# Stick-breaking attention values: one 512-column matmul per key block in place of two of 256

## The chip, the cores and the metric

The kernel runs on one core of a Trainium2 chip. The metric is the device time of one execution in microseconds (us); the time before is the median of three runs. A core has five engines that work beside each other: PE (TensorE) multiplies matrices, DVE (VectorE) and ACT (ScalarE) do elementwise work, POOL (GpSimd) does elementwise work that need not read PSUM, and SP issues transfers. PEld is the loading of the stationary operand into PE, which the profile keeps apart from the matmuls (PE). PSUM is the memory that PE writes its sums to; SBUF is the working memory that all engines read.

## What is computed

One layer of a decoder: a feed-forward half step, a mixing step of two groups of heads side by side (HGRN2, a gated recurrence, and stick-breaking attention), an output projection, and a second feed-forward half step. The sequence is 1024 tokens behind 16 meta tokens, the width is 1024. The change is in the stick-breaking attention (8 heads of 64), which is strictly causal:

```python
z = einsum('bhqd,bhkd->bhqk', qblk, k) * scale
log_beta = where(allowed, log_sigmoid(z), -inf)
log_keep = where(allowed, log_sigmoid(-z), 0.0)
suffix = cumsum(log_keep, axis=3, reverse=True) - log_keep
w = exp(log_beta + suffix)
out = einsum('bhqk,bhkd->bhqd', w, v)
```

The last line is the part that changes: the weights `w` times the values `v`.

## The kernel before

Products that need more precision than one pass gives are made from two parts of each operand, a high part (a cast to the type float32r) and a low part (what the cast left over): high times high, high times low and low times high are summed, low times low is left out where it can be.

**The jobs.** The attention is cut into 32 jobs: 8 heads, and in each head four jobs of two query blocks of 128 (`b0` = 0, 6, 2, 4 is a job's first query block). A job has three lists of steps, each with a number that stands for its length on PE:

- `score`: the scores of a query block against its keys (tile `z`, lines 1205 to 1208), sigmoids on ACT (`keep`, `sig`), the suffix products by a scan on DVE (`keep`, line 1215), the weights by a multiplication on POOL (`sig`, line 1220);
- `turn`: PE transposes of the weights, one group of up to four key blocks at a time, into PSUM (tile `flip`, lines 1069 and 1118, two buffers). ACT casts each group to its high part and DVE subtracts for the low part (`sb_parts`, lines 1183 and 1184), into `wu` (groups of real keys) or `wm` (the 16 meta keys). A transpose into a buffer of `flip` waits until DVE has read that buffer;
- `value`: one step for each of the job's `b0` + 3 key blocks. The loaded operand `v` has 128 columns, 64 with the high part of the head's values and 64 with the low part. The high weights, 256 columns wide, move past all 128 columns (line 1139); the low weights move past the 64 high columns alone (line 1141). The sum `oacc` lies in PSUM, 256 columns wide; its partitions 0 to 63 have high times high and low times high, 64 to 127 have high weights times low values.

At a job's last key block `sb_out` takes the sum out: ACT copies partitions 64 to 127 (`olow`, line 1176), and one DVE addition of 64 x 256 (`ot`, line 1177) adds them to partitions 0 to 63. In each second head `put_split` then cuts the result into its parts (`ohi` on ACT, `olo` on POOL) and stores it.

**The order.** PE's order is as the program writes it. `braid` writes it in rounds: each round takes up a new job; a job's `turn` steps come two rounds and its `value` steps three rounds later. For each round the lengths of all its steps are summed, and blocks of other PE work (`fill`) are set between them until they come to 1.22 times that sum. The fill is 64 blocks of 12 matmuls each of the HGRN2 projections (tile `proj`, lines 160 to 162, 272, 384 or 512 columns wide). What is left of it runs after the last job. On DVE, ACT, POOL and SP the scheduler of the framework sets the order. Below, a block means one of these.

Of the kernel before, what the change touches and what calls it, by code (L numbers as in the profile page):

```python
# [11 lines left out]
F32 = mybir.dt.float32  # L12
F32R = mybir.dt.float32r
# [7 lines left out]
P = 128  # L21
# [3 lines left out]
META = 16  # L25
# [14 lines left out]
class Block:  # L40
# [1031 lines left out]
    def sb_jobs(self, keys, fetch, pool):  # L1072


        nc = self.nc
        qD, kD, vD, oD = keys
        pools = pool
        heads = [(p, hh) for p in range(4) for hh in range(2)]
        kept = {}

        def load(p, hh):
            rows = slice(64 * hh, 64 * hh + 64)
            qs = fetch.tile([P, SEQ], F32R, tag="qs", name="qs", bufs=2)
            ks = [fetch.tile([P, T], F32R, tag=f"ks{i}", name="ks", bufs=2) for i in range(2)]
            for i in range(2):
                part = slice(64 * i, 64 * i + 64)
                nc.sync.dma_start(qs.bitcast(F32)[part], qD[p, rows, i])
                for j in range(2):
                    nc.sync.dma_start(ks[j].bitcast(F32)[part], kD[p, rows, j])
            return qs, ks  # L1090

        def load_v(p, hh):
            v = fetch.tile([P, 9, P], F32R, tag="v", name="v", bufs=2)
            nc.sync.dma_start(v.bitcast(F32), vD[p, :, :, hh * P : (hh + 1) * P])
            return v

        def job(p, hh, qs, ks, v, b0):
            sigs, acc, wm, wu = [], [], [], []
            score, turn, value = [], [], []
            for bi in range(2):  # L1100
                score += self.sb_scores(pool, qs, ks, b0 + bi, sigs)

            def unit(u, bi):
                if bi == 0 or b0 == 4 * u - 1:
                    wu.append([
                        pool.tile([P, 4, 256], F32R, tag=f"wu{i}", name="wu", bufs=3)
                        for i in range(2)
                    ])
                spans = [(META + P * j, P) for j in range(4 * u, min(4 * u + 4, b0 + bi + 1))]
                ps = self.flip(sigs[bi], spans)  # L1110
                self.sb_parts([t[:, : len(spans), bi * P : (bi + 1) * P] for t in wu[u]], ps)

            def meta():
                wm.extend(kept["wm"][0])
                kept["wm"].reverse()
                ps = self.ptr.tile([META, 2, P], F32, tag="tr", name="flip")
                for bi in range(2):
                    nc.tensor.transpose(ps[:, bi, :], sigs[bi][:, :META], self.ident)
                self.sb_parts([t[:META] for t in wm], ps)

            for bi in range(2):
                for u in range(-(-(b0 + bi + 1) // 4)):
                    n = min(4, b0 + bi + 1 - 4 * u)
                    turn.append((107 * n, lambda u=u, bi=bi: unit(u, bi)))
            turn.append((214, meta))

            def values(j):
                if j == 0:
                    acc.append(self.po.tile([P, 256], F32, tag="o", name="oacc"))
                o = acc[0]  # L1130
                if j == b0 + 2:
                    w = [t.rearrange("p b t -> p (b t)") for t in wm]
                    vj, c = v[:, 0], slice(0, 256)
                else:
                    c = slice(128, 256) if j == b0 + 1 else slice(0, 256)
                    w = [t[:, j % 4, c] for t in wu[j // 4]]
                    vj = v[:, 1 + j]
                end = j == b0 + 2
                nc.tensor.matmul(o[:, c], vj, w[0], start=j == 0, stop=False,  # L1139
                                 skip_group_check=True)  # L1140
                nc.tensor.matmul(o[:64, c], vj[:, :64], w[1], start=False, stop=end,  # L1141
                                 skip_group_check=True)
                if end:
                    self.sb_out(p, hh, b0, o, kept, pool, oD)

            for j in range(b0 + 3):
                value.append((240, lambda j=j: values(j)))
            return score, turn, value

        kept["wm"] = [[fetch.tile([P, 2, P], F32R, name=f"wm{j}{i}") for i in range(2)]  # L1150
                      for j in range(2)]
        for t in chain(*kept["wm"]):
            nc.vector.memset(t.bitcast(F32), 0.0)
        none = kept["wm"][1][1].rearrange("p b t -> p (b t)").bitcast(F32)[META:]
        for p in range(4):
            nc.sync.dma_start(vD[p, META:, 0], none)
        ahead, v = load(*heads[0]), load_v(0, 0)
        yield None
        pool = pools[0]
        for i, (p, hh) in enumerate(heads):  # L1160
            qs, ks = ahead
            if i:
                v = load_v(p, hh)
            for b0 in (0, 6, 2, 4):
                if b0 == 2 and i + 1 < len(heads):
                    ahead = load(*heads[i + 1])
                yield job(p, hh, qs, ks, v, b0)

    def sb_out(self, p, hh, b0, o, kept, pool, oD):

        nc = self.nc
        if hh == 0 and b0 == 0:
            kept["o"] = pool.tile([P, SEQ], F32, tag="ot", name="ot")
        s = slice(b0 * P, b0 * P + 256)
        t = pool.tile([P, 256], F32, tag="olow", name="olow", bufs=2)
        nc.scalar.copy(t[64:], o[64:])
        nc.vector.tensor_add(kept["o"][64 * hh : 64 * hh + 64, s], o[:64], t[64:])
        if hh == 1:
            self.put_split(oD, p, s, kept["o"][:, s], pool)

# [643 lines left out]
```

## Time and profile before

| | before |
|---|---|
| three runs | 2082.09, 2081.91, 2078.43 us; median 2081.91 |
| the profiled execution's own time | 2077.59 us |
| its span | 2075.9 us |
| granted clock of PE, mean | 0.998 |
| the jobs lie at | about 914 to 1203 us of the span |
| high-weight matmuls into `oacc` | 160 from `wu` (32 of them 128 columns wide), 32 from `wm` |
| low-weight matmuls into `oacc` | as many |

The sum on the page counts every instruction's busy time, and matmuls overlap each other: a matmul of 256 columns is shown with 0.28 us, but the next can start about 0.11 us later. What a matmul costs in a row of others is therefore read from the distance between starts, not from its duration. "Idle" in brackets behind an instruction is the time that its engine stood still before it by the profile, with the work that ended it.

### The profile page before, as it was taken

To read this page: it belongs to the slowest core of one execution; us is meant where nothing else is said; L and a number is where in the kernel's file an instruction comes from. 1 tells how busy PE (TensorE), PEld (TensorE's weight loads), DVE (VectorE), ACT (ScalarE), POOL (GpSimd) and SP (SyncE) were. 2 spreads that over 40 slices of the span, in tenths; PEclk is the share of its full clock that TensorE was granted. 3 is DMA by queue.
4 is the path that set the end of the run, shared out by engine and by line. 5 is a ranking of instruction groups with operands and counts; after the bars stand their busy time and mean duration, and the time that the engine had idled before them with its cause. 6 is when DMAs were issued, how large, how long until landed. Compare 5 with 4: busy or idle time off the path is not lost.

```text
span 2075.9 us, 31597 instructions
## 1 busy us (share of the span) xinstructions
PE 2005.5 (97%) x11249; PEld 1782.6 (86%) x11249; DVE 1382.7 (67%) x2073; ACT 901.6 (43%) x1858; POOL 632.4 (30%) x696
## 2 busy tenths in 40 slices
PE   6999999999999999999999998999899999999999
PEld 6999999999987899888887878877788888878887
DVE  6867745556688842258878767658667667667774
ACT  7633333334564534466666614336233323334443
POOL 2266635452000002243333300211545445431000
PEclk9999999999999999999999999999999999999999
DMA  7643322226875646435453153683333333239573
GB/s 218 209 141 106 115 84 90 98 79 228 285 231 168 212 134 181 147 109 139 120 143 113 59 212 101 204 270 117 103 100 112 94 105 112 91 135 352 192 228 112
DMA packets 287535, 313.90 MB, mean 151 GB/s; under 512 B 24017, under 2 KB 215889, under 8 KB 287377
## 3 DMA queue, kind: packets, MB, share of 16 engines
q1 hardware_dynamic: 270192, 259.78, 40.6%
q0 software_dynamic: 16144, 52.10, 6.6%
q8 instruction: 89, 1.46, 0.3%
q14 instruction: 70, 0.57, 0.1%
q10 hardware_dynamic: 1040, 0.00, 0.0%
HBM read 227.57 MB, written 84.23 MB: 150 GB/s over the span
## 4 chain that ended last, share of the span: by engine, by line
PE 77%; DVE 6%; ACT 2%; DMA 2%; issue 2%; POOL 0%; SPq 0%; DVEq 0%; ACTq 0%; POOLq 0%
PE o L597 17%; PE qb L313 13%; PE qc L313 8%; PE qa L313 8%; PE proj L160 5%; PE proj L162 5%; PE proj L161 5%; PE qd L313 3%; PE o L559 3%; PE wo L1250 3%; PE flip L1069 2%; PE lvl L838 1%; DVE keep L1215 1%; PE oacc L1139 1%; PE oacc L1141 1%
## 5 line engine op out<-in xcount | busy, mean ns | idle before, releaser
L313 PE MATMUL qb<-T,wh 128*128 128x384 f32 (+1 forms) x1056 | 319.5, 363 | 6.9 <-DVE u L359 6.8
L270 DVE TENSOR_TENSOR wl<-s,wh 128x512 fp32r<-128x512 f32 x176 | 200.7, 1141 | 96.3 <-ACT wh L268 92.1
L313 PEld LDWEIGHTS qb<-T,wh 128*128 128x128 f32 x1056 | 195.8, 188 | 31.9 <-ACT wh L268 9.2
L313 PE MATMUL qa<-B,wh 128*128 128x384 f32 (+1 forms) x704 | 216.0, 369 | 3.1 <-DVE sg L421 2.8
L597 PE MATMUL o<-wl,th 128*128 128x512 f32 x539 | 209.6, 390 | 3.0 <-DVE wl L518 2.9
L597 PE MATMUL o<-wh,tl 128*128 128x512 f32 x539 | 209.5, 390 | 0.7 <-DVE tl L518 0.7
L597 PE MATMUL o<-wh,th 128*128 128x512 f32 x539 | 209.9, 391 | 0.0
L270 DVE TENSOR_TENSOR wl<-raw,wh 128x512 fp32r<-128x512 f32 x184 | 171.1, 932 | 52.5 <-ACT wh L268 48.9
L160 PE MATMUL proj<-xh,wh 128*128 128x384 f32 (+2 forms) x576 | 205.0, 356 | 0.2 <-ACT xh L250 0.2
L268 ACT CAST wh<-s 128x512 fp32r<-128x512 f32 x176 | 109.3, 622 | 220.0 <-PE qb L313 174.7
L161 PE MATMUL proj<-xh,wl 128*128 128x384 f32 (+2 forms) x576 | 199.2, 346 | 0.0
L162 PE MATMUL proj<-xl,wh 128*128 128x384 f32 (+2 forms) x576 | 198.9, 345 | 0.1
L268 ACT CAST wh<-raw 128x512 fp32r<-128x512 f32 x184 | 113.8, 621 | 194.5 <-PE qc L313 107.0
L313 PE MATMUL qb<-T,wl 128*128 128x384 f32 (+1 forms) x528 | 191.9, 363 | 1.8 <-DVE wl L270 1.8
L516 ACT CAST th<-act 128x512 fp32r<-128x512 f32 (+2 forms) x176 | 96.6, 550 | 177.2 <-PE o L597 121.1
L518 DVE TENSOR_TENSOR tl<-act,th 128x512 fp32r<-128x512 f32 (+2 forms) x176 | 106.1, 606 | 64.2 <-ACT th L516 62.5
L313 PEld LDWEIGHTS qa<-B,wh 128*128 128x128 f32 x704 | 131.2, 189 | 19.9 <-DVE sg L421 3.2
L313 PE MATMUL qd<-X,wh 128*128 128x272 f32 x704 | 144.3, 292 | 1.7 <-DVE X L679 1.7
L283 POOL TENSOR_TENSOR s<-raw 128x512 f32<-128x512 f32 x88 | 119.4, 1357 | 82.1 <-DVE wl L270 64.9
L1215 DVE TENSOR_TENSOR_SCAN keep<-keep 128x144 f32<-128x144 f32 (+6 forms) x112 | 127.1, 1138 | 6.5 <-ACT keep L1211 4.3
L1220 POOL TENSOR_TENSOR sig<-sig,keep 128x144 f32<-128x144 f32 (+3 forms) x64 | 86.3, 1349 | 144.7 <-DVE keep L1215 84.5
L313 PE MATMUL qa<-B,wl 128*128 128x384 f32 (+1 forms) x352 | 129.3, 367 | 0.3 <-DVE wl L270 0.3
(341 smaller groups left out, 4762.2 us busy)
## 6 DMA issues: line engine op xcount, KB each, us to landing
raw<-in_ffn_w_in_dram SPq DMA_DIRECT2D x224, 256.0 KB, 3.0
raw<-in_ffn_w_out_dram SPq DMA_DIRECT2D x176, 256.0 KB, 4.3
raw<-in_w_in_dram SPq DMA_DIRECT2D x28, 512.0 KB, 4.4
ks<-kD SPq DMA_DIRECT2D x32, 260.0 KB, 5.3
oT<-oD SPq DMA_DIRECT2D x32, 256.0 KB, 4.7
ak<-in_ffn_w_out_dram SPq DMA_DIRECT2D x22, 256.0 KB, 5.1
v<-vD SPq DMA_DIRECT2D x8, 576.0 KB, 5.0
vD<-vhl SPq DMA_DIRECT2D x8, 512.0 KB, 3.5
```

Of the source, the lines that this page charges most:

```text
L160: nc.tensor.matmul(ps, wh[:, s], xs, start=k == 0, stop=False)
L161: nc.tensor.matmul(ps, wl[:, s], xs, start=False, stop=False)
L162: nc.tensor.matmul(ps, wh[:, s], xl[:, k, c0 : c0 + n], start=False, stop=k == nk - 1)
L268: nc.scalar.copy(hi, src)
L270: nc.vector.tensor_sub(lo, src, hi.bitcast(F32))
L283: op(t, x, y)
L313: nc.tensor.matmul(ps, a[:, k, :], b[:, k0 + k, :], start=start and k == 0 and i == 0, stop=k == 3 and i == 2, skip_group_check=True,)
L516: nc.scalar.copy(hi, src)
L518: nc.vector.tensor_sub(lo, src, hi.bitcast(F32))
L597: nc.tensor.matmul(banks[bank][m], z[:, m * P : (m + 1) * P], y, start=start and q == 0 and e == 0, stop=q == nq - 1 and e == 2, skip_grou ...
L1215: nc.vector.tensor_tensor_scan(out=kv, data0=kv, data1=kv, initial=1.0 if last else keep[:, end : end + 1], op0=ALU.mult, op1=ALU.bypass,)
L1220: nc.gpsimd.tensor_mul(sig, sig, keep[:, 1 : nk + 1])
```

## The change

The high and low parts of a group's weights now lie side by side in one tile (`wu` has a dimension of 2 between the key block and the 256 columns, `wm` likewise). For each key block the loaded `v` (all 128 columns) stays, and both parts move past it in one matmul of 2 x 256 columns. `oacc` becomes 2 x 256 columns wide (2 KB in each partition; it was 1 KB). The low weights now meet the low values as well; that product lands in `oacc[64:, 1]` and isn't read. At the eviction three pieces are summed: `o[:64, 0]`, the copy of `o[64:, 0]`, and `o[:64, 1]`, so there is a second DVE addition for each job. The length that `braid` counts for a `value` step goes from 240 to 228.

```diff
             def unit(u, bi):
                 if bi == 0 or b0 == 4 * u - 1:
-                    wu.append([
-                        pool.tile([P, 4, 256], F32R, tag=f"wu{i}", name="wu", bufs=3)
-                        for i in range(2)
-                    ])
+                    wu.append(
+                        pool.tile([P, 4, 2, 256], F32R, tag="wu", name="wu", bufs=3)
+                    )
...
-                self.sb_parts([t[:, : len(spans), bi * P : (bi + 1) * P] for t in wu[u]], ps)
+                c = slice(bi * P, bi * P + P)
+                self.sb_parts([wu[u][:, : len(spans), i, c] for i in range(2)], ps)
...
             def values(j):
                 if j == 0:
-                    acc.append(self.po.tile([P, 256], F32, tag="o", name="oacc"))
+                    acc.append(self.po.tile([P, 2, 256], F32, tag="o", name="oacc"))
                 o = acc[0]
...
+                c = slice(128, 256) if j == b0 + 1 else slice(0, 256)
                 end = j == b0 + 2
-                nc.tensor.matmul(o[:, c], vj, w[0], start=j == 0, stop=False,
-                                 skip_group_check=True)
-                nc.tensor.matmul(o[:64, c], vj[:, :64], w[1], start=False, stop=end,
+                w, vj = (wm[0], v[:, 0]) if end else (wu[j // 4][:, j % 4], v[:, 1 + j])
+                nc.tensor.matmul(o[:, :, c], vj, w[:, :, c], start=j == 0, stop=end,
                                  skip_group_check=True)
...
             for j in range(b0 + 3):
-                value.append((240, lambda j=j: values(j)))
+                value.append((228, lambda j=j: values(j)))
...
-        nc.scalar.copy(t[64:], o[64:])
-        nc.vector.tensor_add(kept["o"][64 * hh : 64 * hh + 64, s], o[:64], t[64:])
+        nc.scalar.copy(t[64:], o[64:, 0])
+        out = kept["o"][64 * hh : 64 * hh + 64, s]
+        nc.vector.tensor_add(out, o[:64, 0], t[64:])
+        nc.vector.tensor_add(out, o[:64, 1], out)
```

Three places show what this does to the order. The first is PE in the first head, between two transposes of a job. Before:

```order
L1139 MATMUL oacc<-wm_9468,v 128x256
L1141 MATMUL oacc<-wm_9469,v 64x256
L1205 MATMUL z<-ks,qs 128x348
L1206 MATMUL z<-ks,qs 128x348
L1118 MATMUL flip<-ident,sig 16x128 x2
L1139 MATMUL oacc<-wu,v 128x256
L1141 MATMUL oacc<-wu,v 64x256
L1069 MATMUL flip<-ident,sig 128x128
```

And now:

```order
L1136 MATMUL oacc<-wm_9468,v 128x512
L1201 MATMUL z<-ks,qs 128x348
L1202 MATMUL z<-ks,qs 128x348
L1118 MATMUL flip<-ident,sig 16x128 x2
L1136 MATMUL oacc<-wu,v 128x512
L1069 MATMUL flip<-ident,sig 128x128
```

Each pair has become one matmul of twice the columns, and nothing else moved here.

The second place is DVE around the eviction of a job, where the trace of before stands at 958 to 963 us. `wl` is the low part of a column of projection weights, `keep` the scan. Before:

```order
L147 TENSOR_TENSOR wl<-raw,wh 128x1024
L1184 TENSOR_TENSOR wm_9469<-flip,wm_9468 16x256
L1215 SCALAR_TENSOR_TENSOR keep<-keep 128x263
L1177 TENSOR_TENSOR ot<-oacc,olow 64x256
L1215 SCALAR_TENSOR_TENSOR keep<-keep 128x329
L1184 TENSOR_TENSOR wu<-flip,wu 128x4x128
L1184 TENSOR_TENSOR wu<-flip,wu 128x3x128
```

And now:

```order
L1180 TENSOR_TENSOR wm_9468<-flip,wm_9468 16x256
L1211 SCALAR_TENSOR_TENSOR keep<-keep 128x263
L1172 TENSOR_TENSOR ot<-oacc,olow 64x256
L1211 SCALAR_TENSOR_TENSOR keep<-keep 128x329
L1173 TENSOR_TENSOR ot<-oacc,ot 64x256
L1180 TENSOR_TENSOR wu<-flip,wu 128x4x128
L147 TENSOR_TENSOR wl<-raw,wh 128x1024
L1180 TENSOR_TENSOR wu<-flip,wu 128x3x128
```

The second addition (L1173) stands ahead of the subtraction that gives PE its `flip` buffer back, and here `wl` has gone from the front to behind that subtraction.

The third place is PE in the middle of the attention, where the trace of before stands at 1031 us (the same is found once more, at 1102 us). Of the 12 matmuls of the block the first three are shown. Before:

```order
L1069 MATMUL flip<-ident,sig 128x128 x4
L1139 MATMUL oacc<-wu,v 128x256
L1141 MATMUL oacc<-wu,v 64x256
L160 MATMUL proj<-xh,wh 128x512
L161 MATMUL proj<-xh,wl 128x512
L162 MATMUL proj<-xl,wh 128x512
...
L1069 MATMUL flip<-ident,sig 128x128 x3
L1205 MATMUL z<-ks,qs 128x328
L1206 MATMUL z<-ks,qs 128x328
L1139 MATMUL oacc<-wu,v 128x128
L1141 MATMUL oacc<-wu,v 64x128
```

And now:

```order
L1069 MATMUL flip<-ident,sig 128x128 x4
L1136 MATMUL oacc<-wu,v 128x512
L1069 MATMUL flip<-ident,sig 128x128 x3
L1201 MATMUL z<-ks,qs 128x328
L1202 MATMUL z<-ks,qs 128x328
L1136 MATMUL oacc<-wu,v 128x2x128
L160 MATMUL proj<-xh,wh 128x512
L161 MATMUL proj<-xh,wl 128x512
L162 MATMUL proj<-xl,wh 128x512
```

The block that stood between two groups of transposes stands behind the second group now; the block that followed the next group before has moved on by one place in the same way.

More of the change, by code (lines that the diff above doesn't have):

```diff
@@ L1104, in unit @@
                 if bi == 0 or b0 == 4 * u - 1:
-                    wu.append([
-                        pool.tile([P, 4, 256], F32R, tag=f"wu{i}", name="wu", bufs=3)
-                        for i in range(2)
-                    ])
+                    wu.append(
+                        pool.tile([P, 4, 2, 256], F32R, tag="wu", name="wu", bufs=3)
+                    )
                 spans = [(META + P * j, P) for j in range(4 * u, min(4 * u + 4, b0 + bi + 1))]
                 ps = self.flip(sigs[bi], spans)
-                self.sb_parts([t[:, : len(spans), bi * P : (bi + 1) * P] for t in wu[u]], ps)
+                c = slice(bi * P, bi * P + P)
+                self.sb_parts([wu[u][:, : len(spans), i, c] for i in range(2)], ps)
             def meta():
-                wm.extend(kept["wm"][0])
+                wm.append(kept["wm"][0])
                 kept["wm"].reverse()
@@ L1118, in meta @@
                     nc.tensor.transpose(ps[:, bi, :], sigs[bi][:, :META], self.ident)
-                self.sb_parts([t[:META] for t in wm], ps)
+                self.sb_parts(
+                    [wm[0][:META, i].rearrange("p (b t) -> p b t", b=2) for i in range(2)], ps
+                )
             for bi in range(2):
@@ L1128, in values @@
                 if j == 0:
-                    acc.append(self.po.tile([P, 256], F32, tag="o", name="oacc"))
+                    acc.append(self.po.tile([P, 2, 256], F32, tag="o", name="oacc"))
                 o = acc[0]
[L1131 to L1137, printed above, removed]
+                c = slice(128, 256) if j == b0 + 1 else slice(0, 256)
                 end = j == b0 + 2
-                nc.tensor.matmul(o[:, c], vj, w[0], start=j == 0, stop=False,
-                                 skip_group_check=True)
-                nc.tensor.matmul(o[:64, c], vj[:, :64], w[1], start=False, stop=end,
+                w, vj = (wm[0], v[:, 0]) if end else (wu[j // 4][:, j % 4], v[:, 1 + j])
+                nc.tensor.matmul(o[:, :, c], vj, w[:, :, c], start=j == 0, stop=end,
                                  skip_group_check=True)
@@ L1146, in job @@
             for j in range(b0 + 3):
-                value.append((240, lambda j=j: values(j)))
+                value.append((228, lambda j=j: values(j)))
             return score, turn, value
-        kept["wm"] = [[fetch.tile([P, 2, P], F32R, name=f"wm{j}{i}") for i in range(2)]
-                      for j in range(2)]
-        for t in chain(*kept["wm"]):
+        kept["wm"] = [fetch.tile([P, 2, 256], F32R, name=f"wm{j}") for j in range(2)]
+        for t in kept["wm"]:
             nc.vector.memset(t.bitcast(F32), 0.0)
-        none = kept["wm"][1][1].rearrange("p b t -> p (b t)").bitcast(F32)[META:]
+        none = kept["wm"][1][:, 1].bitcast(F32)[META:]
         for p in range(4):
```

## The prediction

> **What bounds the kernel now.** I read the page first, for which engine fills the span and where the changed lines stand in the chain that ended last.
>
> ```profile
> PE 2005.5 (97%) x11249; PEld 1782.6 (86%) x11249; DVE 1382.7 (67%) x2073; ACT 901.6 (43%) x1858; POOL 632.4 (30%) x696
> ...
> PE o L597 17%; PE qb L313 13%; PE qc L313 8%; PE qa L313 8%; PE proj L160 5%; PE proj L162 5%; PE proj L161 5%; PE qd L313 3%; PE o L559 3%; PE wo L1250 3%; PE flip L1069 2%; PE lvl L838 1%; DVE keep L1215 1%; PE oacc L1139 1%; PE oacc L1141 1%
> ```
>
> PE is busy almost always, and the two changed lines have about 1% each of the chain, some 40 us. So the change works on what sets the end; it lies in one stage, though. The view by stages shows that stage:
>
> ```profile
> 920.00:1000.00 80.00, 75.02 (x499) 67.02 (x498) 66.25 (x92) 49.94 (x127) 33.46 (x44) 1.00 0.42 116
> 1000.00:1100.00 100.00, 93.70 (x610) 83.10 (x610) 81.33 (x110) 61.46 (x155) 34.89 (x48) 1.00 0.46 123
> 1100.00:1203.00 103.00, 97.65 (x639) 86.86 (x638) 76.52 (x110) 60.63 (x153) 34.92 (x45) 1.00 0.30 89
> ```
>
> The columns after the length are PE, PEld, DVE, ACT and POOL busy, the granted clock, and the transfers. In these 283 us PE is busy for 266.4 (75.02 + 93.70 + 97.65) and stands still for 16.6. DVE is busy for 224.1, 79%. The clock is full. The view of waits, for PE alone in this stage, tells what the 16.6 us are:
>
> ```profile
> PE flip L1069 <- DVE wu L1184: 11.9, 19, 2.3
> PE flip L1118 <- DVE wu L1184: 2.8, 3, 1.3
> PE flip L1069 <- DVE wm L1184: 1.8, 4, 0.5
> ```
>
> All but 0.1 us of it are transposes that wait until DVE has read the buffer that they write: 26 waits, 16.5 us. So two things can change the time here: how long PE's own row of matmuls takes, and how late DVE is with those subtractions.
>
> **The change part by part.** *One matmul of 512 columns for two of 256.* Distances between starts tell what a matmul costs in a row:
>
> ```profile
> 934.43 0.36 PE L1139 MATMUL oacc<-wu,v 128*128 128x256 f32 x1
> 934.63 0.28 PE L1141 MATMUL oacc<-wu,v 128*64 128x256 f32 x1
> 934.75 0.28 PE L1139 MATMUL oacc<-wu,v 128*128 128x256 f32 x1
> 934.86 0.28 PE L1141 MATMUL oacc<-wu,v 128*64 128x256 f32 x1
> 934.97 0.28 PE L1139 MATMUL oacc<-wu,v 128*128 128x256 f32 x1
> ...
> 935.20 0.40 PE L160 MATMUL proj<-xh,wh 128*128 128x512 f32 x1
> 935.43 0.39 PE L161 MATMUL proj<-xh,wl 128*128 128x512 f32 x1
> 935.66 0.40 PE L162 MATMUL proj<-xl,wh 128*128 128x512 f32 x1
> ...
> 941.00 0.48 PE L160 MATMUL proj<-xh,wh 128*128 128x512 f32 x1
> 941.32 0.39 PE L161 MATMUL proj<-xh,wl 128*128 128x512 f32 x1
> ```
>
> From 934.75 to 935.20 run two pairs: 0.225 us a pair. From 935.20 to 935.66 run two matmuls of 512 columns: 0.23 each. Where a matmul of another kind stands ahead, the pair takes 934.43 to 934.75, 0.32, and a wide one 941.00 to 941.32, 0.32. A wide matmul costs what the pair costs, within the 0.01 us of the rows. There are 192 pairs (160 from `wu`, 32 from `wm`); at 0.005 us either way that is 0, between -1.0 and +1.0 us. I take 0.
>
> By the Trainium skill ("TensorE: Matmul & The Clock Gate", Back-to-back issue gap) a matmul of N columns takes N / 2.4 + 2.5 ns, so a pair is 218.3 and a wide one 215.8 ns, and 192 of them would give back an estimated 0.5 us. The rows, 225 and 230 ns, do not show that gain; they decide, and either figure leaves the sum as it is within its bounds.
>
> The weight loads that go, and the addition that comes, have these rows (smallest, median and largest duration in ns):
>
> ```profile
> L1141 PEld LDWEIGHTS oacc<-wu,v x160: 133/138/139, 923.7 to 1200.9; 128*64 128x64 f32 x160
> ...
> L1177 DVE TENSOR_TENSOR ot<-oacc,olow x32: 417/417/420, 933.7 to 1202.0; 64x256 f32<-64x256 f32 x32
> ```
>
> *192 weight loads fewer*: 192 x 0.138 = 26.5 us of PEld. They lie beside the matmul ahead of them: with 0.14 us of loading for each second start, starts still come every 0.11 us. I count them at 0.
>
> *The wait for both parts.* One matmul now waits for ACT's cast and DVE's subtraction together, where the first could start on the cast alone. No row of PE's waits above names the value matmuls, so the parts are there before they are needed: 0. Behind such a wait would stand all of PE.
>
> *The second addition*: 32 x 0.417 = 13.3 us more on DVE, whose share in the stage goes from 79% to (224.1 + 13.3) / 283 = 84%. It can cost from nothing, if it always falls into DVE's idle time, to 13.3 us, if each one makes PE wait. Queued behind it on DVE are scans and the subtractions that free PE's buffers. How many of PE's waits have an eviction's addition in the unbroken run of DVE work that ended them? I went through the 26. It is 8. The first:
>
> ```profile
> 950.32 0.40 DVE L1184 TENSOR_TENSOR wu<-flip,wu 128x256 fp32r<-128x256 f32 x1
> 950.75 0.42 DVE L1177 TENSOR_TENSOR ot<-oacc,olow 64x256 f32<-64x256 f32 x1
> 951.20 0.94 DVE L1215 TENSOR_TENSOR_SCAN keep<-keep 128x347 f32<-128x347 f32 x1
> 952.06 0.39 DVE L1184 TENSOR_TENSOR wm<-flip,wm 16x256 fp32r<-16x256 f32 x1
> ```
>
> DVE goes from `wu` to `wm` without a pause, and PE's transpose starts at 952.59 when `wm` is done. One more addition here makes that 953.01. PE's side of the first of the 8, of four others that the change touches, and of the last:
>
> ```profile
> 952.59 0.30 PE L1069 MATMUL flip<-ident,sig 128*128 128x128 f32 x1 [0.46 <-DVE wm L1184]
> 963.13 0.41 PE L1069 MATMUL flip<-ident,sig 128*128 128x128 f32 x2 [0.71 <-DVE wu L1184]
> ...
> 1026.03 0.41 PE L1069 MATMUL flip<-ident,sig 128*128 128x128 f32 x2 [0.47 <-DVE wm L1184]
> ...
> 1096.76 0.41 PE L1069 MATMUL flip<-ident,sig 128*128 128x128 f32 x2 [0.46 <-DVE wm L1184]
> ...
> 1143.89 0.30 PE L1069 MATMUL flip<-ident,sig 128*128 128x128 f32 x1 [2.27 <-DVE wu L1184]
> ...
> 1177.92 0.30 PE L1069 MATMUL flip<-ident,sig 128*128 128x128 f32 x1 [0.19 <-DVE wu L1184]
> ```
>
> *The moved blocks* (a value step counts 228 instead of 240). No block is added or lost: 192 x 12 x 1.22 / 1000 = 2.8 us less is owed over the stage, and one block of 512 columns (12 x 0.23 = 2.8 us) runs after the last job instead of within. What moves is which waits a block covers. Ahead of 1026.03 and 1096.76 stands a block now: those two waits go (-0.9), and with them what the addition would add there. At 963.13 DVE's split of projection weights has gone behind the subtraction, so that this wait goes too (-0.7). At 1143.89 a block of 512 columns takes the place of one of 272, and the split has gone: of 2.27 us I take 2.2 off. Late next: at the third place shown ahead of this, and its twin, the order is now transposes of four, three, a block, four, four again, then the meta keys, with no block between the last groups. The block's 2.8 us is the most that its cover is worth; the least is 0; the waits of this stage lie between 0.2 and 2.3, so I take the middle of them, rounded up, 1.5 for each of the two places: +3.0 (0 to 5.6). So four of the 8 waits keep their added addition: 4 x 0.42 = +1.7.
>
> *The eviction's chain*: the result reaches the store 0.42 us later in a job. ACT's cast and POOL's subtraction behind it serve a store, and none of PE's waits above names either of them: 0. The tiles `wu`, `wm` and `oacc` keep their number of buffers, and `oacc` is freed 0.42 us later, with the next job's first sum going to the other buffer: 0.
>
> **The sum**: 0 - 0.9 - 0.7 - 2.2 + 3.0 + 1.7 = +0.9 us. It is made against the profiled execution (span 2075.9, own time 2077.59), which lies 4.3 us under the median of the three runs and 0.8 under their lowest. Set on the median: 2081.91 + 0.9 = 2082.8 us. What a measurement of this kernel can tell from no change is 0.2%, 4.2 us; the three runs themselves span 3.7. So I forecast no change that can be told.
>
> **The rivals.** *DVE's additions reach PE (slower).* The mechanism is the second addition in DVE's queue ahead of the subtractions that free `flip`. For it: all of PE's idle time in the stage ends on DVE, and POOL and ACT wait on DVE's scans too. Against: only 8 of 26 waits have such an addition in their run. The moved blocks alone come to -0.8 (-0.9 - 0.7 - 2.2 + 3.0); each addition that comes through in full adds 0.42 to that. It decides at 12 of the 32: 12 x 0.42 - 0.8 = +4.2. Waits that are none today, because DVE is just in time, are what could bring the number there. With 20 it is +7.6, 2089.5 us, and I take that as its far end.
>
> *The moved blocks cover more than they uncover (faster).* If the two uncovered places cost nothing and the freed ones give all of it, the sum is -0.9 - 0.7 - 2.2 + 1.7 = -2.1; with the additions falling into idle time as well it is -3.8, and with the 1.0 us of PE's own row -4.8: 2077.1 us. For it: such waits hang on a few tenths of a us each. Against: the cover is only shifted.
>
> *The weight loads bind (faster).* If PE waited for its loads, the 26.5 us of loads that go would come off: 2055.4 us. Against: the starts every 0.11 us above. The Trainium skill ("Perfetto Trace Analysis", Identifying the Most-Contended Engine) judges PE by the busy share of its weight loads rather than by that of its matmuls, and by this measure, 86%, removing loads is worth while; that starts here follow at one distance, whether a load of 64 or of 128 columns lies between them, speaks against it.
>
> *The change does not do what it says*: that a matmul over two runs of 128 columns (32 of them), or one that fills 2 KB of PSUM, is slower than the pair. At 0.05 us on each of 192 it would be +9.6. No row has such a form; the 512-column `proj` fills 2 KB at 0.23 us and speaks against it for the rest. I count it with the slower cases.
>
> **How the numbers follow.** No change within 0.2%: 0.67. Slower, by DVE's additions 0.16 and by the wide matmul 0.03: 0.19. Faster, by the blocks 0.12 and by the loads 0.02: 0.14. The range takes in the far ends of the two likelier rivals, short of the last half us of the slower one: 2077 to 2089 us. The likeliest case alone lies within 2078 to 2086.
>
> **What would show it.** Right: a wide matmul follows another after 0.23 us, as the pair did; PEld loses some 26 us in the stage while PE's busy time there changes by what overlaps in the display alone; DVE gains 13 us; PE's waits still all end on DVE, 26 or so of them with a sum near 16.5 us; those at 1026, 1096 and 1143 us are gone, and new ones stand near 1036 and 1107. Wrong: waits for DVE that sum to over 20 us, or a wide matmul whose successor starts after 0.25 us or more, make it slower; a sum of waits under 12 us makes it faster.

## The result, and the profile after

| | before | after |
|---|---|---|
| median, lowest to highest of 14 runs each | 2081.26 us, 2075.86 to 2084.63 | 2085.12 us, 2081.32 to 2088.65 |
| time after / before | 1 | 1.0025 [1.0017, 1.0033] |
| profiled execution: own time, span | 2077.59, 2075.9 us | 2081.32, 2079.6 us |
| from the first score matmul to the first transpose after the jobs' stage | 305.8 us | 311.8 us |

The kernel became slower by 0.25%, some 5 us by the ratio and 3.9 by the medians. That is just beyond what I called no change (0.2%, which the interval takes in), and within the range of the prediction. The last row of the table is worked out from the starts below: the first score matmul (`z`) before and after, and the first transpose of the next stage (`flip` from `vT`) before and after, from the timeline of PE.

```profile
909.42 0.34 PE L1205 MATMUL z<-ks,qs 128*128 128x144 f32 x1
...
1215.23 0.97 PE L1069 MATMUL flip<-ident,vT 128*16 128x128 f32 x6
```

```profile
909.00 0.34 PE L1201 MATMUL z<-ks,qs 128*128 128x144 f32 x1
...
1220.80 1.30 PE L1069 MATMUL flip<-ident,vT 128*16 128x128 f32 x9
```

So the stage of the change is 6.0 us longer, and the rest of the profiled execution 2.3 us shorter. The rest holds no changed code; 1.5 us of its difference is told in the last section. What PE waits for in the stage, from the view of waits of the kernel after (us in total, times, longest):

```profile
PE flip L1069 <- DVE wu L1180: 18.3, 21, 1.9
PE flip L1069 <- DVE wm L1180: 2.1, 3, 1.1
PE flip L1118 <- DVE wu L1180: 1.4, 2, 0.8
```

It is still the transposes that wait for DVE, now 21.8 us where it was 16.5. Of the 6.0 us, 5.3 are these waits, and about 1.5 is a stretch of half clock at 1149.76 us, shown further down. What is left, -0.8 us, is not traced to a place. The sums over the stage, in the same windows as before (columns: length; busy time of PE, PEld, DVE, ACT, POOL; granted clock; transfers):

```profile
920.00:1000.00 80.00, 74.41 (x445) 63.66 (x444) 69.33 (x100) 50.02 (x127) 32.60 (x42) 1.00 0.42 115
1000.00:1100.00 100.00, 92.02 (x540) 78.00 (x539) 83.33 (x120) 61.81 (x157) 34.48 (x49) 1.00 0.44 119
1100.00:1203.00 103.00, 94.43 (x544) 80.31 (x543) 79.68 (x121) 60.46 (x149) 32.04 (x44) 0.98 0.30 89
```

DVE rises from 224.1 to 232.3 us, 82% of these 283 us. PE is busy for 260.9 us of them in place of 266.4: it stands still for 22.1 us, where it was 16.6. (The windows end at 1203 us, and the stage now ends later. From the first score matmul to the first transpose after the stage DVE rises from 235.0 to 246.0 us, and PE from 288.3 to 288.8.) The changed instructions themselves, by the view of the tile `oacc` and, in the last row, of the tile `ot` (smallest, median and largest duration in ns):

```profile
L1136 PE MATMUL oacc<-wu,v x160: 277/398/505, 923.1 to 1203.7; 128*128 128x512 f32 x128, 128*128 128x256 f32 x32
...
L1172 DVE TENSOR_TENSOR ot<-oacc,olow x32: 415/417/421, 933.2 to 1205.1; 64x256 f32<-64x256 f32 x32
```

```profile
L1173 DVE TENSOR_TENSOR ot<-oacc,ot x32: 386/416/419, 934.6 to 1205.5; 64x256 f32<-64x256 f32 x32
```

The second addition costs DVE what the first does, 32 x 0.416 = 13.3 us.

### The profile page after: what moved, and what is told of

The parts are those of the page before. It is cut to its first block, busy times and chain, and to the rows that moved or that the text cites. A ratio compares the mean times of both kernels' runs of the same rounds, so it can differ in the third digit from the quotient of the medians.

```text
span 2079.6 us, 31241 instructions
## 1 busy us (share of the span) xinstructions
PE 2004.0 (96%) x11057; PEld 1770.9 (85%) x11057; DVE 1388.4 (67%) x2103; ACT 902.8 (43%) x1858; POOL 629.2 (30%) x696
## 4 chain that ended last, share of the span: by engine, by line
PE 77%; DVE 7%; ACT 2%; issue 2%; DMA 1%; POOL 0%; DVEq 0%; SPq 0%; ACTq 0%; POOLq 0%
PE o L597 17%; PE qb L313 13%; PE qc L313 8%; PE qa L313 8%; PE proj L160 5%; PE proj L162 5%; PE proj L161 5%; PE qd L313 3%; PE o L559 3%; PE wo L1246 3%; DVE keep L1211 2%; PE flip L1069 2%; PE lvl L838 2%; PE oacc L1136 1%; DVE wu L1180 1%
```

## The experiments

Three theories stand behind the expectations below. A: the second DVE addition delays the subtractions that free `flip`. B: the moved blocks of other PE work (the value step's 228 in place of 240) uncover waits. C: the wide matmul costs more than the pair did. Since each part can be made alone, the first four kernels are the combinations that separate them. Each edit is against the kernel after, except where the text says before. Narrow means the pair of matmuls, wide the one of 512 columns.

**The wide matmul with the old block order.** The value step's number goes back to 240.

```diff
-                value.append((228, lambda j=j: values(j)))
+                value.append((240, lambda j=j: values(j)))
```

> The changed kernel with the old length of a value step (240), so that the blocks stand between the same transposes as before the change, and all else as changed (wide matmul, second addition). Theory A, the second addition on DVE makes the time: it stays slower than the kernel before by 3 to 6 us, and PE's waits for DVE in the jobs sum to 19 us or more. Theory B, the moved blocks make it: it comes back to the kernel before within 1.5 us, with waits of 16 to 18 us. Theory C, the wide matmul makes it: slower by 5 us with waits near 16.5 us.

Measured: 2087.68 us, ratio 1.0035 [1.0022, 1.0049]. In its profile the stage takes 309.1 us and PE waits 20.4 us for DVE. With the old block order nothing is gained back, so the blocks are not all of it. The time is what theory A expected or a little more (7.1 us by the medians, for 3 to 6), and so are the waits.

**The new block order alone.** The kernel before, with its pair of matmuls and its one addition, gets the number 228.

```diff
-                value.append((240, lambda j=j: values(j)))
+                value.append((228, lambda j=j: values(j)))
```

> The kernel before with the new length of a value step (228) alone: pairs of narrow matmuls, one addition at an eviction, and the blocks where the change puts them. Theory A (the second addition): as the kernel before within 1.5 us. Theory B (the moved blocks): slower by 3 to 6 us, waits of PE for DVE 20 us or more. Theory C (the wide matmul): as the kernel before.

Measured: 2082.36 us, ratio 1.0006 [0.9996, 1.0016]: not to be told from before. Its stage takes 307.8 us in the profile, 2.0 more than before, with 18.3 us of waits. The timeline of PE shows three of them:

```profile
1052.42 0.63 PE L1069 MATMUL flip<-ident,sig 128*128 128x128 f32 x4 [1.21 <-DVE wu L1184]
...
1057.76 0.30 PE L1069 MATMUL flip<-ident,sig 128*128 128x128 f32 x1 [1.04 <-DVE wu L1184]
...
1177.78 0.63 PE L1069 MATMUL flip<-ident,sig 128*128 128x128 f32 x4 [1.61 <-DVE wu L1184]
```

Before, the first two transposes did not wait, and the third waited 0.19 us. The moved blocks alone open these places; what they close elsewhere (1026, 1096, most of 1143.89) nearly pays for it.

**One addition with the new block order.** The second addition is left out, and with it `o[:64, 1]`, the low weights times the high values.

```diff
-        nc.vector.tensor_add(out, o[:64, 1], out)
```

> The changed kernel without the second addition: high values times low weights are computed and not added to the output. Blocks as changed. Theory A (the second addition): back to the kernel before within 1.5 us. Theory B (the moved blocks): stays 3 to 6 us slower than the kernel before. Theory C (the wide matmul): stays 5 us slower, with waits of PE near 16.5 us.

Measured: 2084.49 us, ratio 1.0018 [1.0008, 1.0027]; stage 308.8 us, waits 19.1 us. By the time this is what theory B expected. Theory C expected such a time as well, but with waits near 16.5 us. The kernel lies 0.0012 above the narrow one of the same order, with intervals that overlap, and 1.0 us above it in the stage. Its profile has a stretch of half clock there, at 1150.05 us, and that of the narrow one has none; such a stretch costs about 1.5 us (last section). So this difference does not speak for theory C.

**One addition with the old block order.** Both edits together (240, and the second addition left out).

> The wide matmul alone: blocks as before the change, and no second addition (high values times low weights are computed and not added to the output). Theory A and theory B: as the kernel before within 1.5 us, waits near 16.5 us. Theory C (the wide matmul): slower by about 5 us.

Measured: 2078.01 us, ratio 0.9991 [0.9982, 1.0000]; stage 303.2 us, waits 15.2 us. This kernel has every wide matmul of the change and none of its other parts, and it is not slower than before: theory C falls. The cells side by side:

| | 240 | 228 |
|---|---|---|
| narrow, one addition | 1 (before) | 1.0006 [0.9996, 1.0016] |
| wide, one addition | 0.9991 [0.9982, 1.0000] | 1.0018 [1.0008, 1.0027] |
| wide, two additions | 1.0035 [1.0022, 1.0049] | 1.0025 [1.0017, 1.0033] (after) |

With the old blocks, the addition costs 0.0044, some 9 us, of which 5.9 lie in the stage by the profiles; with the new ones 0.0007, which is within the two intervals, and 3.0 us in the stage. The new blocks cost 0.0027 with one addition and nothing with two. The two causes don't add: with the old blocks the addition delays twelve transposes, with the new ones six, as shown next.

The two kernels with 240 have the same order on PE, so their starts can be laid side by side. From the first to the last value matmul, the one with two additions falls 5.9 us behind, 5.7 of them in twelve steps of 0.30 to 0.82 us, each at a transpose into `flip`. At one of them, DVE in the kernel with one addition:

```profile
995.54 0.42 DVE L1172 TENSOR_TENSOR ot<-oacc,olow 64x256 f32<-64x256 f32 x1
995.99 1.51 DVE L1210 TENSOR_TENSOR_SCAN keep<-keep 128x329 f32<-128x329 f32 x1
997.42 1.12 DVE L1179 TENSOR_TENSOR wu<-flip,wu 128x512 fp32r<-128x512 f32 x2
...
998.23 0.63 PE L1069 MATMUL flip<-ident,sig 128*128 128x128 f32 x4 [0.37 <-DVE wu L1179]
```

and in the one with two additions:

```profile
995.15 0.42 DVE L1172 TENSOR_TENSOR ot<-oacc,olow 64x256 f32<-64x256 f32 x1
995.60 1.51 DVE L1211 TENSOR_TENSOR_SCAN keep<-keep 128x329 f32<-128x329 f32 x1
997.14 0.42 DVE L1173 TENSOR_TENSOR ot<-oacc,ot 64x256 f32<-64x256 f32 x1
997.59 1.38 DVE L1180 TENSOR_TENSOR wu<-flip,wu 128x512 fp32r<-128x512 f32 x2
...
998.43 0.63 PE L1069 MATMUL flip<-ident,sig 128*128 128x128 f32 x4 [0.96 <-DVE wu L1180]
```

(The last row of each is PE's.) The addition stands between the scan and the subtraction, DVE has no pause, and the wait grows from 0.37 to 0.96 us, by 0.59. At another of the twelve there was no wait to grow: with one addition the transpose at 1056.96 us starts at once, with two it waits:

```profile
1058.32 0.30 PE L1069 MATMUL flip<-ident,sig 128*128 128x128 f32 x1 [0.66 <-DVE wu L1180]
```

The two kernels with 228 also share PE's order: there the addition comes through at six places, 2.7 us in all.

**A third addition.** Wide, 240, and one more addition of the same size at each eviction, whose result nothing reads.

```diff
-                value.append((228, lambda j=j: values(j)))
+                value.append((240, lambda j=j: values(j)))
...
         nc.vector.tensor_add(out, o[:64, 1], out)
+        nc.vector.tensor_add(t[:64], o[:64, 1], t[64:])
```

> Length 240 with the wide matmul and a third DVE addition of the same size at each eviction (into an unread half of the copy's tile). Theory A (each addition in DVE's queue delays the subtractions that PE waits for): some 3 to 6 us slower again than the same kernel with two additions, so 2090 to 2095 us, and PE's waits for DVE 4 us longer than there. Rival (the order in which the scheduler puts DVE's work, not its amount, makes the time): within 1.5 us of the kernel with two additions, 2087 us.

Measured: 2093.59 us, ratio 1.0056 [1.0043, 1.0069]; stage 316.1 us. The waits of PE:

```profile
PE flip L1069 <- DVE wu L1181: 11.3, 22, 1.6
PE flip L1069 <- DVE wm L1181: 6.2, 5, 1.5
PE flip L1069 <- POOL olo L1004: 4.4, 4, 1.9
PE flip L1118 <- DVE wu L1181: 1.6, 2, 1.0
```

With one, two and three additions the ratio is 0.9991, 1.0035 and 1.0056, and the stage 303.2, 309.1 and 316.1 us: it follows the dose, also when some 3 us are taken off the last for two stretches of half clock (1028.40 and 1151.28 us), which the other two have not. The 4.4 us that the view puts down to POOL's `olo` are DVE's too. At each of the four places PE starts 0.146 or 0.147 us after the end of DVE's subtraction, as at nearly all of its waits for DVE; POOL's `olo`, which no transpose reads, happened to end in between. With them PE waits for DVE 23.5 us, 3.1 more than with two additions, where 4 were expected.

**The same sum with one DVE addition.** Wide, 240, the full result: ACT copies the third piece and POOL adds it.

```diff
-        nc.scalar.copy(t[64:], o[64:, 0])
-        out = kept["o"][64 * hh : 64 * hh + 64, s]
-        nc.vector.tensor_add(out, o[:64, 0], t[64:])
-        nc.vector.tensor_add(out, o[:64, 1], out)
+        rows = slice(64 * hh, 64 * hh + 64)
+        out = kept["o"][rows, s]
+        nc.scalar.copy(t[rows], o[64:, 0])
+        nc.scalar.copy(out, o[:64, 1])
+        nc.vector.tensor_add(t[rows], o[:64, 0], t[rows])
+        nc.gpsimd.tensor_add(out, out, t[rows])
```

> Length 240 with the wide matmul and all three pieces summed, but with one DVE addition at an eviction: ACT copies two pieces (one more copy of 0.37 us) and POOL makes the last addition. Theory A (the second DVE addition is the cost): 2078 to 2081 us, as the wide matmul with one addition, since PE's waits end on DVE. Rival (any added work in the chain of an eviction costs as much, as ACT's casts go before DVE's subtractions): 2084 to 2088 us.

Measured: 2084.89 us, ratio 1.0016 [1.0008, 1.0025]; stage 307.6 us, waits for DVE 16.4 us and for POOL 0.8. Taking the addition off DVE gives back 4.0 of the 5.2 us of waits that it had brought to PE in the kernel with two. The time remains above before, though: it lies in the range of the rival (2084 to 2088) and not in that of theory A (2078 to 2081), so the waits bear theory A out here and the time does not.

The profile tells where the time is. In the jobs' stage it lies 1.8 us above before, and one stretch of half clock makes 1.5 of that: from 1148.35 us twelve `proj` matmuls of 384 columns take 3.73 us, and the same twelve 2.18 in the kernel with one addition. Most of the rest of the profile's excess lies in the next stage, where three more such stretches begin (1274.92, 1285.16 and 1380.73 us, the last of double length). The other runs agree: their mean granted clock is 0.9952, and that of the runs of before beside them 0.9970; among the runs of before a clock lower by 0.001 goes with some 1.2 to 1.7 us more, so by this estimate 2 to 3 us of its excess go with the clock.

**The addition alone.** The kernel before, with one more addition at each eviction, whose result nothing reads.

```diff
         nc.vector.tensor_add(kept["o"][64 * hh : 64 * hh + 64, s], o[:64], t[64:])
+        nc.vector.tensor_add(t[:64], o[:64], t[64:])
```

> The kernel before with one more DVE addition of the same size at each eviction, whose result nobody reads; pairs of narrow matmuls, old blocks. PE's order is that of the kernel before, and DVE's after the jobs too. Theory A (the addition alone makes the time): slower by 4 to 7 us, PE's waits for DVE 20 us or more. Rival (it is the addition together with the later stage's changed DVE order, or the wide layout): within 2 us of the kernel before.

Measured: 2085.41 us, ratio 1.0019 [1.0009, 1.0029], 4.0 us. The view of waits:

```profile
PE flip L1069 <- DVE wu L1185: 12.4, 20, 2.3
PE flip L1069 <- DVE wm L1185: 3.2, 4, 0.9
PE flip L1118 <- DVE wu L1185: 2.8, 3, 1.3
```

The time is what theory A expected (4 to 7 us); the waits sum to 18.4 us, where 20 were expected. This is the kernel before in every other respect, with PE's order unchanged, and the addition alone makes it slower by nearly what the whole change does. In the profile, six transposes start later by 0.29 to 0.45 us each, 2.2 us in all, and 1.4 us more go at one place, where the clock falls to half; that is told below. The stage is 309.6 us, 3.8 more than before. The added work does not stand where the change has it: here both additions are ahead of DVE's scan of 329 columns (seven places), and with the change the second stands behind it, as in the rows above. Of the twelve late transposes in the wide kernel with two additions and 240, five start within 4.1 us of such a scan's start; here no transpose that does so is late. The last section shows why.

No kernel that gives the full result was faster than before.

## Why the prediction was right and wrong

The range held; the likeliest case was too low, and the time came out just past the edge of no change, at the side where I had put 0.19. The range held because it took in the slower rival. Of +0.9 us that the sum made, the profile shows +6.0 in the stage, and the ratio of the runs 5.2. By the stages of the experiments the way from before to after is +2.0 for the blocks alone, +1.0 for the wide matmul added to that (with a stretch of half clock of 1.5 in it), and +3.0 for the addition. Step by step:

**The wide matmul, taken at 0: right.** Three in a row after a transpose, and the block behind them, in the kernel after:

```profile
933.89 0.94 PE L1136 MATMUL oacc<-wu,v 128*128 128x512 f32 x3
934.67 0.40 PE L160 MATMUL proj<-xh,wh 128*128 128x512 f32 x1
934.91 0.39 PE L161 MATMUL proj<-xh,wl 128*128 128x512 f32 x1
```

Three wide matmuls take 0.78 us from start to start; the three pairs at the same place took 0.77 (934.43 to 935.20). The experiment with the wide matmul alone sets the whole part at -0.0009, with an interval that ends at 1.

**The weight loads, taken at 0: right.** The 192 loads of 64 columns are gone, and the wide matmul with nothing else, 0.9991, gives back less than 0.2%. The rival by which loads bind PE would have given 2055 us. The Trainium skill ("Perfetto Trace Analysis", Identifying the Most-Contended Engine) takes the busy share of weight loads as a measure of PE's headroom; in this kernel it misleads, since PEld is busy for 15.0 us less in the three windows (237.0 before, 222.0 after) and PE gains nothing by it. Over the whole stage it is 10.1 us less (253.7 and 243.6). I had expected 26 us there; the busy time counts loads that overlap only once.

**The wait for both parts and the eviction's chain, taken at 0: right.** Neither a value matmul nor anything of the store stands among PE's waits of the kernel after. (With the wide matmul and the old order, one value matmul waits 0.2 us.)

**The second addition, taken at +1.7: the first term that was mis-sized.** I counted only waits that stood in the trace, 8 of 26, and gave four of them 0.42 us. The two kernels with 228 show six places and 2.7 us: the four that I had kept grow by 1.8 (952.57, 998.57, 1134.00 and 1180.88 us in the kernel after), and two that did not wait without the addition (963.49 and 1069.61) bring 0.9. The two with 240 show twelve, which is the number from which I had said that this rival decides. The step that failed is that the sum lets only waits of today grow; the rival named the places where DVE is just in time, and the sum put them at nothing without a look. Such places, as at 1056.96 us, can be seen in the profile of before only by the gap between the end of DVE's subtraction and the start of PE's transpose, and I had not listed these gaps.

**The moved blocks, taken at -0.8: the second, and the larger.** With the narrow pair they make +2.0 us in the stage, and 0.0006 by the runs, which is not to be told from nothing. What I predicted for the places that I looked at came: the waits at 1026 and 1096 are gone, that of 2.27 us at 1143.89 too, and new ones stand near 1036 and 1107, at 0.85 and 0.84 us where I took 1.5. What I missed are the places that I had not gone through. In the kernel after, by the timeline of PE:

```profile
1038.24 0.52 PE L1069 MATMUL flip<-ident,sig 128*128 128x128 f32 x3 [0.85 <-DVE wu L1180]
...
1052.53 0.63 PE L1069 MATMUL flip<-ident,sig 128*128 128x128 f32 x4 [1.69 <-DVE wu L1180]
...
1057.88 0.30 PE L1069 MATMUL flip<-ident,sig 128*128 128x128 f32 x1 [1.10 <-DVE wu L1180]
...
1149.60 0.74 PE L1069 MATMUL flip<-ident,sig 128*128 128x128 f32 x3 [1.95 <-DVE wu L1180]
...
1180.88 0.63 PE L1069 MATMUL flip<-ident,sig 128*128 128x128 f32 x4 [1.94 <-DVE wu L1180]
```

At 1052.53 a block of 272 columns had stood between a group of one and a group of four; it has gone behind the second, as at the two places that I did price. At 1057.88 a block of 384 has moved on in the same way. At 1149.60 the 2.27 us of 1143.89 has come back two groups later: a split of projection weights (`wl`) now stands ahead of the subtraction there. At 1180.88 PE's order is as before; it is DVE's that has changed:

```profile
1171.19 2.52 DVE L147 TENSOR_TENSOR wl<-raw,wh 128x1024 fp32r<-128x1024 f32 x1
...
1179.74 0.39 DVE L1173 TENSOR_TENSOR ot<-oacc,ot 64x256 f32<-64x256 f32 x1
1180.06 1.13 DVE L1180 TENSOR_TENSOR wu<-flip,wu 128x512 fp32r<-128x512 f32 x2
```

From the `wl` on, DVE works without a pause until the transpose can start, 9.7 us later. I had looked for `wl` right ahead of each wait, and not ten microseconds upstream. With the narrow pair the same three waits come to 1.21, 1.04 and 1.61 us, so they belong to the blocks for the most part, and not to the addition.

**The rival that came true** is the first, DVE's additions, together with the part of the blocks that I had priced as a gain. I gave slower by over 0.2% a chance of 0.19, and took no case in which both went wrong at once.

**The signs that I named.** A sum of waits over 20 us was to make it slower: it is 21.8. DVE was to gain 13 us: the rows of the addition make 13.3, the windows show 8.2, and the whole stage 11.0. What is missing there went to the splits `wl` and others, which took less time in this run (last section).

**What stays open.** The old blocks with two additions have a median 7 us over before, of which 3.3 lie in the stage by the profile; most of the rest lies in the next one (up to about 1435 us, 5.8 us longer in the profile), where the scheduler of the framework sets DVE's rows in another order although no code there changed. Two stretches of half clock begin there (1277.82 and 1383.63 us), which before has not. That order, and the clock, differ from kernel to kernel, and no run here separates them. For the kernel after this part of the profile is 0.4 us shorter than before.

## What to carry to other kernels

Work that is added to an engine off the critical path is not priced by the waits that the trace shows, but by the slack of every handover to the bound engine: list the handovers that are just in time as well, and look a whole unbroken run upstream of each. Where in that engine's queue the work stands decides how much of it comes through. When a number that places filler work is changed, go through every place at which filler stood between a producer and the waiting engine, and not only those that catch the eye. Merging two matmuls into one that streams the same columns saved nothing on the bound engine here, and the piece that it added for another engine to collect had to be paid for.

## What the runs showed of the hardware

**A wait costs more when it empties a slice of the clock's window.** In the kernel after, the windows around the wait of 1.95 us (columns as above; the eighth value is the granted clock):

```profile
1146.35:1149.76 3.41, 1.46 (x10) 0.91 (x9) 3.38 (x4) 2.25 (x6) 0.65 (x2) 1.00 0.02 6
1149.76:1153.17 3.41, 3.41 (x17) 3.41 (x17) 3.23 (x6) 0.94 (x3) 1.67 (x2) 0.50 0.52 154
```

PE was busy for 1.46 of 3.41 us, and for the next 3.41 us its clock is 0.50. From the transposes at 1149.60 to the value matmul behind the block it takes 3.72 us, and through the same matmuls 2.22 us in the kernel with the new block order alone, whose clock stays full there. So the stretch costs about 1.5 us. The kernel after, and then the other:

```profile
1153.32 0.87 PE L1136 MATMUL oacc<-wu,v 128*128 128x512 f32 x3
```

```profile
1148.12 0.52 PE L1069 MATMUL flip<-ident,sig 128*128 128x128 f32 x3 [1.26 <-DVE wu L1184]
...
1150.34 0.28 PE L1139 MATMUL oacc<-wu,v 128*128 128x256 f32 x1
```

In the kernel before with the added addition it is the same at 1100 us, with matmuls of 512 columns 0.43 us apart in place of 0.23:

```profile
1101.21 0.63 PE L160 MATMUL proj<-xh,wh 128*128 128x512 f32 x1
1101.64 0.63 PE L161 MATMUL proj<-xh,wl 128*128 128x512 f32 x1
```

The starts of such stretches within one profile lie whole multiples of 3.413 us apart (in the kernel with three additions 36, 77, 106 and 126 of them). Laid on that grid, of all nine profiles the four slices of the jobs' stage in which PE was busy for less than 1.6 us were each followed by half clock, and of some twenty with 1.6 to 1.9 us two were. The grid lies differently in each run: the longer wait of before, 2.27 us at 1143.89, fell across two slices, and the clock stayed full:

```profile
1139.22:1142.63 3.41, 2.41 (x21) 2.26 (x19) 3.35 (x5) 3.09 (x9) 1.22 (x3) 1.00 0.78 228
1142.63:1146.05 3.42, 2.15 (x17) 2.02 (x18) 3.26 (x6) 1.88 (x5) 1.92 (x2) 1.00 0.80 234
```

The Trainium skill ("TensorE: Matmul & The Clock Gate", What's actually happening) states a free-running window of 3413 ns, which the multiples bear out; it asks for a whole idle window before the clock falls, where here a window that was 43% busy was enough. So about 1.5 us of the 6 in the profile are a matter of where the grid lay; and the profile of before has such a stretch at 1442.99 us, in a later stage, at a cost of 1.5 us beside the same matmuls of the one of after, which has none there.

**The same instruction on DVE takes different times.** The split `wl` took 1.23 us at 1048.99 and 2.52 at 1171.19 in the kernel after, with the same shape. By the view of lines from 920 to 1203 us, before and after (busy us, mean ns; then the idle time ahead):

```profile
L147 DVE TENSOR_TENSOR wl<-raw,wh 128x1024 fp32r<-128x1024 f32 x12 | 20.4, 1699 | 4.2 <-ACT wh L145 3.4 <-DMA oD<-olo 0.7
```

```profile
L147 DVE TENSOR_TENSOR wl<-raw,wh 128x1024 fp32r<-128x1024 f32 x12 | 16.9, 1411 | 2.4 <-ACT wh L145 1.7 <-DMA oD<-olo 0.7
```

The same twelve instructions take 3.5 us less after. POOL's multiplication (`sig`) goes with it. In the nine profiles 27 of these splits start while it runs: 18 of them end 1.08 us after its end (1.079 to 1.085) and take up to 3.0 us, and the other nine take 1.20 and are done before it. Four such long splits fall into the profile of before, and two into that of after. The scan of 329 columns does the same: 61 of the 63 that start during the multiplication end 0.70 us after its end (0.695 to 0.703). The kernel before, and behind it the one with the added addition:

```profile
995.97 1.12 POOL L1220 TENSOR_TENSOR sig<-sig,keep 128x528 f32<-128x528 f32 x1 [2.56 <-DVE keep L1215]
...
996.28 1.51 DVE L1215 TENSOR_TENSOR_SCAN keep<-keep 128x329 f32<-128x329 f32 x1
```

```profile
998.58 1.12 POOL L1221 TENSOR_TENSOR sig<-sig,keep 128x528 f32<-128x528 f32 x1 [1.71 <-DVE keep L1216]
...
999.34 1.06 DVE L1216 TENSOR_TENSOR_SCAN keep<-keep 128x329 f32<-128x329 f32 x1
```

The added addition lets the scan start later, and the scan ends 0.70 us after POOL all the same: it takes 1.06 to 1.19 us in place of 1.51 at all seven places where an eviction's addition stands ahead of it. So an addition ahead of this scan cost PE nothing, and one behind it, as in the change, comes through. What the two engines share there, these traces do not tell.
